# Modulation mat-vecs of a two-block network: one VectorE multiply-and-sum instruction per weight block in place of a GpSimd multiply and a ScalarE accumulating copy

## The chip, the cores and the metric

The kernel runs on one core of a Trainium2 chip. The metric is the device time of one execution in microseconds; the median of several runs is given.

## What is computed

Two transformer-like blocks over 512 tokens of width 1024, batch 1, all in float32. The first block has two layers of three sublayers (swiglu feed-forward, a mixer, swiglu feed-forward), the second has two layers (attention, then a squared-ReLU feed-forward) and carries 256 context tokens beside the 512. Every sublayer is modulated by columns that come from a conditioning vector:

```python
c_act = jax.nn.silu(c)
for l in range(DEPTH):                                   # first block
    mod = (c_act @ ada_w[l] + ada_b[l]).reshape(b, N_SUB, 3, 1, D_MODEL)
    h = modulate(x, mod[:, 0, 0], mod[:, 0, 1])          # x * (1 + scale) + shift
    y = swiglu_ffn(h, ffn1_w_in[l], ffn1_w_out[l])
    x = layer_norm(ALPHA * x + 0.5 * mod[:, 0, 2] * y, ln_g[l, 0], ln_b[l, 0])
    ...
for i in range(DEPTH):                                   # second block
    mod_lat = (silu_c @ w_ada[i] + b_ada[i])[:, None, :]
    mod_ctx = silu_cc @ w_ada[i] + b_ada[i]
    ...
```

A modulation vector of 1024 entries is one product of a vector with a 1024x1024 matrix. The change is about how these mat-vecs are computed.

## The kernel before

Activations lie feature-major: 1024 features are 8 tiles of 128 partitions by 512 tokens, kept as a pair of float32r parts (`hh`, `hl`) that add up to the float32 value. Every product is three matmuls (L322 to L324): high with high, high with low, low with high. Weights stream in blocks of 128x1024 float32 (512 KB): SyncE's queue issues the DMA into `raw`, ScalarE casts it to `hi` (L284), VectorE subtracts to get `lo` (L286; for a few blocks GpSimd does). The stream runs three blocks ahead of its use, with five places for split blocks.

The swiglu sublayers, FF1 to FF4 in order of time, have 22 tiles of hidden features in chunks of 2, 4, 4, 4, 4 and 4. A hidden tile takes two weight blocks and 48 matmuls into `pgu` (two PSUM tiles of two banks); ScalarE makes the silu `sg`, VectorE the product `gf` (the gate product), and `gf` is split into `gh` and `gl`. A chunk then goes through the output weights: eight `po` tiles (two PSUM banks), and for each a residual update `z` on VectorE (L635).

The modulation weights come as blocks `araw` of 128 output features by 1024 inputs. `ada` is a generator whose steps `ffn` takes between its hidden tiles. A step issues the DMA of one block from ScalarE's queue (L420, two buffers); for each conditioning vector that uses the block, GpSimd multiplies it with that vector, which lies on all partitions (`crow`), into `amul` (L425, one buffer), and ScalarE copies `amul` onto itself with a sum along the row, which gives one column of the result (L428). There are 224 blocks and 288 mat-vec steps: 56 of them in FF1, 80 in FF2, 88 in FF3 and 64 in FF4. In FF2 to FF4 some blocks of the second block's modulation serve two vectors (`mod` for the sequence, `modc` for the context).

The instructions' order on each engine is not the order of the code: the framework's scheduler sets it when the program is built. `after` adds an order between two instructions of one engine. `self.base` is the last instruction of the norm before, behind which the modulation steps must stay on their engine; before, it is the GpSimd instruction that makes the next residual base (L609).

Of the kernel before, what the change touches and what calls it, by code (L numbers as in the profile page):

```python
# [35 lines left out]
# ---------------------------------------------------------------- layout of the inputs (host, no arithmetic on data)  # L36

class Cols:
    """Small vectors, one array [128, n]: feature j * 128 + p of a vector sits in column off + j."""
# [16 lines left out]
def in_blocks(w):  # L56
    """(K, M) -> [M / 128][128][K / 128 * 128]: the stationary tiles of one block of output features."""
    k, m = w.shape
    return w.reshape(k // P, P, m // P, P).transpose(2, 1, 0, 3).reshape(m // P, P, k)


def out_blocks(w):
    """(chunk of K, 1024) -> [nb][128][1024]: for each block of output features, all k tiles of the chunk."""
    cs = w.shape[0] // P
    nm = KT // cs
    nb = KT // nm
    return w.reshape(cs, P, nb, nm, P).transpose(2, 1, 3, 0, 4).reshape(nb, P, DM)


def tok_blocks(w, kt):  # L70
    """(K, M) -> [K / 128 / kt][128][kt * M]: moving rows for token-major products."""
    k, m = w.shape
    n = k // P // kt
    return w.reshape(n, kt, P, m).transpose(0, 2, 1, 3).reshape(n, P, kt * m)
# [72 lines left out]
def ada_blocks(w):  # L147
    """(depth, 1024, M) -> [depth][M / 1024][8][128][1024]: output features on the partitions."""
# [113 lines left out]
# ---------------------------------------------------------------- the program  # L262

class WeightStream:
    """Streams blocks of weights in the order of their use and splits each exactly into two float32r parts."""
# [30 lines left out]
class Kernel:  # L296
# [3 lines left out]
    # ---------------- small helpers  # L300
# [11 lines left out]
    def split(self, hi, lo, src):  # L312
        """hi + lo = src exactly, both float32r."""
# [3 lines left out]
    def mm3(self, ps, terms, start=True, stop=True):  # L317
        """ps += sum of (a_hi + a_lo)^T (b_hi + b_lo) over the terms."""
# [7 lines left out]
    def dense(self, ps, w, off, x, ks, t0, t1):  # L326
        """ps[128 features, t0:t1] = W^T x for the stationary tiles at w[:, off + i * 128]."""
# [7 lines left out]
    def dense_tok(self, ps, blocks, kpb, m, x, ks, tb):  # L335
        """ps[128 tokens, m] = x^T W for the moving rows in blocks of kpb k tiles."""
# [9 lines left out]
    def quads(self, n, t, name, pool=None, tag="q4", bufs=4):  # L346
        """n pairs (hi, lo) of four feature tiles over t tokens."""
# [12 lines left out]
    def rows(self, t, name):  # L360
        """Eight float32 feature tiles over t tokens, as two groups of four."""
# [5 lines left out]
    def log_exp_table(self):  # L367
        """The activation tables that hold both the logarithm and the exponential, loaded at this point."""
# [3 lines left out]
    def after(self, ins, first):  # L372
        """Keeps ins behind first in their engine's order."""
# [3 lines left out]
    def rsqrt(self, pool, v, n, scale, eps, tag, make=None):  # L377
        """(scale * v + eps) ** -0.5 over [128, n], from logarithm and exponential with a Newton step."""
# [14 lines left out]
    def ps(self, tag, shape, name):  # L393
        """A tile in PSUM: tags a (two of one bank), b (two of two banks), c and d (one bank each)."""
# [6 lines left out]
    # ---------------- modulation  # L401

    def vector(self, row):
        """silu of one of the conditioning vectors, the same on all partitions."""
# [8 lines left out]
    def ada(self, src, vecs, first=None):  # L413
        """Work: src chunk @ silu(vector) + bias, as columns; vecs: list of (row, bias columns, factor, result)."""
        nc = self.nc
        rows = [self.vector(v[0]) for v in vecs]
        for j in range(KT):
# [5 lines left out]
            for row, (_, _, _, res) in zip(rows, vecs):  # L423
                m = self.apool.tile([P, DM], F32, tag="amul", bufs=1, name="amul")
                ins = nc.gpsimd.tensor_tensor(m, w, row, op=ALU.mult)  # L425
                if self.base:
                    self.after(ins, self.base)
                nc.scalar.activation(m, m, AF.Copy, accum_out=res[:, j : j + 1])  # L428
# [5 lines left out]
    def first_norm(self, z, g, b, src, bias):  # L434
        """The norm of the input and the first modulation, whose weights come block by block meanwhile.

        src: blocks of the shift (vector and tensor engines take one each) and of the scale, bias: their columns.
        """
# [23 lines left out]
        def mean(ps, x):  # L462
            """ps = mean of the eight tiles x(m)."""
# [52 lines left out]
    def mod_cols(self, g, b, shift, scale, name):  # L516
        """Columns that take the normalized rows to the next base (ALPHA x) and to the next modulated input."""
# [11 lines left out]
    # ---------------- layer norm (feature-major)  # L529

    def room(self):
        """Space for a norm beside the one that runs in the feed-forward sublayer's."""
        return (self.xpool or self.fpool).tile([P, 7, 256], F32, tag="lb", bufs=1, name="room")

    def layer_norm(self, z, t0, t1, eps, mod, h=None, final=None, behind=None):
        """The norm of z over [t0, t1) in place, in two steps, with the modulated result split into h."""
# [12 lines left out]
        def total(ps, rows, m, eng):  # L549
            """ps = mean over all features, as the rows of 1 or 2 feature tiles from m come in."""  # L550
# [30 lines left out]
        for m in range(KT):  # L581
# [27 lines left out]
            self.base = nc.gpsimd.tensor_scalar(zm, zm, ag, ab, op0=ALU.mult, op1=ALU.add)  # L609
# [4 lines left out]
    # ---------------- feed-forward sublayers  # L614

    def out_steps(self, parts, chunks, last=False, tag="a", before=None):
        """Work: z += gate * (W_out^T x) for chunks of k tiles; parts: (z, gate, x, t, result if not z),
        x one group of k tiles for each chunk.

        With last, by token halves, with before called ahead of each half of the first part.  # L620
        """
# [89 lines left out]
    def mlp(self, parts):  # L711
        """parts: (h, z, gate, t), the tokens of the sequence first, then those of the context, if any."""
# [10 lines left out]
        def inner(part, g, bl, fs):  # L723
            """Two hidden features of the tokens of the context."""
# [48 lines left out]
    # ---------------- mixer of the first block  # L773

    def mixer(self, l, h, out_first):
        nc, tc, ws = self.nc, self.tc, self.ws
        tt, stt, ts = nc.vector.tensor_tensor, nc.vector.scalar_tensor_tensor, nc.vector.tensor_scalar
        with tc.tile_pool(name="mx", bufs=1, reuse_waits="tile") as mp:
# [13 lines left out]
            # -- x B C: projection, causal convolution, silu  # L792
# [20 lines left out]
            # -- dt and f: softplus(u) = max(u, 0) + log1p(exp(-|u|)), token-major  # L813
# [1011 lines left out]
```

## Time and profile before

| | |
|---|---|
| median of 3 runs | 3942.31 us (3937.7 to 3942.68) |
| span of the profiled execution, first to last instruction | 3928.4 us |
| median less that span | 13.9 us |
| TensorE (PE) matmul busy | 3679.7 us, 20206 instructions |
| VectorE (DVE) busy | 2448.7 us |
| ScalarE (ACT) busy | 1843.0 us |
| GpSimd (POOL) busy | 1295.2 us |

The time of the profiled execution itself is not listed apart from the three runs; its span is, and the 13.9 us are what lies around it. A busy share is an average over stages with different limits, so it says where an engine's work is and not what the time hangs on; the chain of waits and the busy time of single stretches say that. Matmuls are pipelined: their rows overlap, and the count of matmuls in a stretch tells their pace better than their durations. PE is the matmul side of TensorE, PEld its weight loads, ACTq and SPq the queues from which ScalarE and SyncE issue DMAs.

### The profile page before, as it was taken

The page shows a single profiled execution, that of the slowest core. Times are in us where ns is not written, and L with a number is a line of the kernel's source. Part 1 is how long each engine was busy: PE and PEld are TensorE (multiplying, and loading weights), DVE is VectorE, ACT ScalarE, POOL GpSimd, SP SyncE. Part 2 cuts the span into 40 slices and gives each one's busy share as a digit, 9 for nine tenths or more (in the row PEclk, how much of TensorE's full clock was granted, in tenths as well). Part 3 has the DMA queues.
Part 4 walks back from the last instruction along what each step waited for, and adds up shares of the span by engine and source line. Part 5 has one row for each costly group of instructions (what it writes and reads, how often), then busy time and mean ns, then how long its engine had stood idle before and what let it go on. Part 6 is the DMA issues. An engine that isn't in the chain of part 4 may idle for free.

```text
span 3928.4 us, 51915 instructions
## 1 busy us (share of the span) xinstructions
PE 3679.7 (94%) x20206; PEld 3171.6 (81%) x20206; DVE 2448.7 (62%) x3699; ACT 1843.0 (47%) x3323; POOL 1295.2 (33%) x888
## 2 busy tenths in 40 slices
PE   7999999999989998989999888999999979989997
PEld 6788877888878887777888787888888868878886
DVE  7664666765676667577656778773333577875445
ACT  3552444555455554435543566452323366744332
POOL 5660313566566663146642212040000221122001
PEclk9999999999999999999999899999999989999998
DMA  6763223376445543124652111011211110112321
GB/s 217 226 221 108 89 68 106 124 233 205 141 153 191 171 129 107 60 97 145 198 194 67 38 38 54 24 54 60 65 60 64 54 58 30 39 49 76 97 92 59
DMA packets 125015, 418.47 MB, mean 107 GB/s; under 512 B 13336, under 2 KB 19224, under 8 KB 124768
## 3 DMA queue, kind: packets, MB, share of 16 engines
q1 hardware_dynamic: 90592, 293.50, 22.8%
q10 hardware_dynamic: 34176, 121.65, 9.6%
q8 instruction: 158, 2.59, 0.3%
q14 instruction: 89, 0.73, 0.1%
HBM read 404.62 MB, written 10.49 MB: 106 GB/s over the span
## 4 chain that ended last, share of the span: by engine, by line
PE 75%; DVE 12%; ACT 5%; POOL 4%; issue 4%; DMA 1%; POOLq 0%; SPq 0%; ACTq 0%; DVEq 0%
PE po L322 8%; PE po L323 8%; PE po L324 8%; PE pgu L323 7%; PE pgu L322 7%; PE pgu L324 7%; PE pm L323 3%; PE pm L322 3%; PE pm L324 3%; POOL amul L425 3%; PE pyo L1168 2%; PE ptt L1154 2%; PE psc L1319 1%; ACT hi L284 1%; DVE lo L286 1%
## 5 line engine op out<-in xcount | busy, mean ns | idle before, releaser
L286 DVE TENSOR_TENSOR lo<-raw,hi 128x1024 fp32r<-128x1024 f32 (+3 forms) x439 | 681.6, 1558 | 404.4 <-ACT hi L284 397.4
L284 ACT CAST hi<-raw 128x1024 fp32r<-128x1024 f32 (+2 forms) x502 | 514.8, 1029 | 861.3 <-PE po L323 455.5
L425 POOL TENSOR_TENSOR amul<-araw,crow 128x1024 f32<-128x1024 f32 x288 | 720.3, 2501 | 406.5 <-ACT amul L428 369.8
L635 DVE SCALAR_TENSOR_TENSOR z<-po,mod,z 128x512 f32<-128x512 f32 (+1 forms) x464 | 300.5, 655 | 489.9 <-PE po L324 488.6
L322 PE MATMUL pgu<-hh,hi 128*128 128x512 f32 (+1 forms) x1536 | 565.8, 373 | 14.6 <-DVE gf L671 6.7
L323 PE MATMUL pgu<-hl,hi 128*128 128x512 f32 (+1 forms) x1536 | 571.6, 373 | 6.1 <-DVE hl L608 4.3
L324 PE MATMUL pgu<-hh,lo 128*128 128x512 f32 (+1 forms) x1536 | 568.7, 371 | 1.9 <-DVE lo L286 1.8
L322 PE MATMUL po<-gh,hi 128*128 128x512 f32 (+1 forms) x1408 | 506.9, 366 | 11.9 <-DVE z L635 11.3
L323 PE MATMUL po<-gl,hi 128*128 128x512 f32 (+1 forms) x1408 | 510.2, 363 | 0.9 <-DVE gl L315 0.9
L324 PE MATMUL po<-gh,lo 128*128 128x512 f32 (+1 forms) x1408 | 509.5, 362 | 0.0
L428 ACT ACTIVATE amul<-amul 128x1024 f32<-128x1024 f32 x288 | 305.6, 1061 | 357.1 <-POOL amul L425 355.8
L286 POOL TENSOR_TENSOR lo<-raw,hi 128x1024 fp32r<-128x1024 f32 (+2 forms) x63 | 154.3, 2452 | 918.9 <-ACT hi L284 827.4
L322 PEld LDWEIGHTS pgu<-hh,hi 128*128 128x128 f32 x1536 | 292.6, 193 | 65.7 <-DVE gf L671 7.4
L323 PEld LDWEIGHTS pgu<-hl,hi 128*128 128x128 f32 x1536 | 295.1, 192 | 58.2 <-DVE hl L608 7.3
L324 PEld LDWEIGHTS pgu<-hh,lo 128*128 128x128 f32 x1536 | 295.5, 192 | 51.4 <-DVE lo L286 3.9
L322 PEld LDWEIGHTS po<-gh,hi 128*128 128x128 f32 x1408 | 268.5, 191 | 54.6 <-DVE z L635 14.6
L323 PEld LDWEIGHTS po<-gl,hi 128*128 128x128 f32 x1408 | 268.8, 191 | 40.6 <-DVE gl L315 1.8
L324 PEld LDWEIGHTS po<-gh,lo 128*128 128x128 f32 x1408 | 268.6, 191 | 40.0
L315 DVE TENSOR_TENSOR gl<-gf,gh 128x512 fp32r<-128x512 f32 (+1 forms) x158 | 165.7, 1051 | 139.6 <-ACT gh L314 139.4
L323 PE MATMUL pm<-hl,hi 128*128 128x512 f32 (+1 forms) x576 | 213.2, 371 | 6.2 <-DVE hl L608 3.9
L322 PE MATMUL pm<-hh,hi 128*128 128x512 f32 (+1 forms) x576 | 210.1, 370 | 4.5 <-ACT hi L284 1.8
L324 PE MATMUL pm<-hh,lo 128*128 128x512 f32 (+1 forms) x576 | 211.5, 370 | 1.8 <-DVE lo L286 1.8
(512 smaller groups left out, 7760.3 us busy)
## 6 DMA issues: line engine op xcount, KB each, us to landing
araw<-in_ada ACTq DMA_DIRECT2D x224, 512.0 KB, 3.5
raw<-in_w SPq DMA_DIRECT2D x128, 512.0 KB, 3.6
raw<-in_f1i SPq DMA_DIRECT2D x88, 512.0 KB, 4.4
raw<-in_f2i SPq DMA_DIRECT2D x88, 512.0 KB, 4.3
raw<-in_mi SPq DMA_DIRECT2D x48, 512.0 KB, 3.3
raw<-in_f1o SPq DMA_DIRECT2D x44, 512.0 KB, 4.3
raw<-in_f2o SPq DMA_DIRECT2D x44, 512.0 KB, 4.4
arawf<-in_ada SPq DMA_DIRECT2D x16, 512.0 KB, 8.6
```

The source lines that it names most:

```text
L284: nc.scalar.copy(hi[:, :n], raw[:, :n])
L286: eng.tensor_tensor(lo[:, :n], raw[:, :n], hi[:, :n].bitcast(F32), op=ALU.subtract)
L315: self.nc.vector.tensor_tensor(lo, src, hi.bitcast(F32), op=ALU.subtract)
L322: mm(ps, ah, bh, start=start and i == 0, stop=False)
L323: mm(ps, ah, bl, start=False, stop=False)
L324: mm(ps, al, bh, start=False, stop=stop and i == n - 1)
L425: ins = nc.gpsimd.tensor_tensor(m, w, row, op=ALU.mult)
L428: nc.scalar.activation(m, m, AF.Copy, accum_out=res[:, j : j + 1])
L635: nc.vector.scalar_tensor_tensor(to, ps, gate[:, m : m + 1], zm, op0=ALU.mult, op1=ALU.add)
L1154: nc.tensor.transpose(pt[:, k, r], pn[:, r, s], self.ident)
L1168: nc.tensor.matmul(out, v[:, kb], x, start=kb == 0 and i == 0, stop=kb == nkb - 1 and i == 1)
L1319: nc.tensor.matmul(ps[:, k0:k1], qt[:, q, q0 : q0 + P], kt[:, k0:k1], start=i == 0, stop=i == 1)
```

## The change

The GpSimd multiply and the ScalarE copy of each step become one `scalar_tensor_tensor` on VectorE: (block x 1.0) x vector, with the row sum written to the result's column. `amul` is still written and read by nobody. The DMA of the blocks stays on ScalarE's queue and keeps its two buffers. `self.base` becomes the VectorE instruction that makes the last low part `hl` of the norm, so that the order between norm and modulation holds on VectorE. Line numbers behind L425 rise by one, behind L609 by two.

```diff
@@ def ada
                 m = self.apool.tile([P, DM], F32, tag="amul", bufs=1, name="amul")
-                ins = nc.gpsimd.tensor_tensor(m, w, row, op=ALU.mult)
+                ins = nc.vector.scalar_tensor_tensor(
+                    m, w, 1.0, row, op0=ALU.mult, op1=ALU.mult, accum_out=res[:, j : j + 1]
+                )
                 if self.base:
                     self.after(ins, self.base)
-                nc.scalar.activation(m, m, AF.Copy, accum_out=res[:, j : j + 1])
@@ def layer_norm
-            self.base = nc.gpsimd.tensor_scalar(zm, zm, ag, ab, op0=ALU.mult, op1=ALU.add)
+            nc.gpsimd.tensor_scalar(zm, zm, ag, ab, op0=ALU.mult, op1=ALU.add)
+            self.base = lo
```

The scheduler orders the program anew. GpSimd and SyncE keep their order but for the multiplies that are gone. Three places show what moves.

VectorE at the start of FF1, behind the last low part `hl` of the first norm. Before:

```order
L286 TENSOR_TENSOR lo<-raw,hi 128x1024 x2
L671 TENSOR_TENSOR gf<-pgu,sg 128x512
L286 TENSOR_TENSOR lo<-raw,hi 128x1024
L315 TENSOR_TENSOR gl<-gf,gh 128x512
L286 TENSOR_TENSOR lo<-raw,hi 128x1024
L671 TENSOR_TENSOR gf<-pgu,sg 128x512
L315 TENSOR_TENSOR gl<-gf,gh 128x512
L286 TENSOR_TENSOR lo<-raw,hi 128x1024
L430 TENSOR_TENSOR mod_85<-mod_85,cols 128x8
```

The same place after the change:

```order
L425 SCALAR_TENSOR_TENSOR amul,mod_85<-araw,crow 128x1024 x6
L286 TENSOR_TENSOR lo<-raw,hi 128x1024
L425 SCALAR_TENSOR_TENSOR amul,mod_85<-araw,crow 128x1024
L286 TENSOR_TENSOR lo<-raw,hi 128x1024
L673 TENSOR_TENSOR gf<-pgu,sg 128x512
L425 SCALAR_TENSOR_TENSOR amul,mod_85<-araw,crow 128x1024
L286 TENSOR_TENSOR lo<-raw,hi 128x1024
L315 TENSOR_TENSOR gl<-gf,gh 128x512
L431 TENSOR_TENSOR mod_85<-mod_85,cols 128x8
L425 SCALAR_TENSOR_TENSOR amul,mod_85<-araw,crow 128x1024
```

Six multiplies stand ahead of the first weight split, and then about two beside each split.

VectorE in the middle of FF3, from one gate product to the next (the ones at 1220.40 and 1229.94 us in the trace of before). Before:

```order
L671 TENSOR_TENSOR gf<-pgu,sg 128x512
L286 TENSOR_TENSOR lo<-raw,hi 128x1024
L315 TENSOR_TENSOR gl<-gf,gh 128x512
L286 TENSOR_TENSOR lo<-raw,hi 128x1024 x2
L671 TENSOR_TENSOR gf<-pgu,sg 128x512
```

After, the first 12 of the 18 rows between the same two products:

```order
L673 TENSOR_TENSOR gf<-pgu,sg 128x512
L431 TENSOR_TENSOR modc<-modc,cols 128x8
L425 SCALAR_TENSOR_TENSOR amul,mod_86<-araw,crow 128x1024
L637 SCALAR_TENSOR_TENSOR z<-po,mod_85,z 128x512
L286 TENSOR_TENSOR lo<-raw,hi 128x1024
L315 TENSOR_TENSOR gl<-gf,gh 128x512
L425 SCALAR_TENSOR_TENSOR amul,modc<-araw,crow 128x1024
L637 SCALAR_TENSOR_TENSOR z<-po,mod_85,z 128x512
L425 SCALAR_TENSOR_TENSOR amul,mod_86<-araw,crow 128x1024
L425 SCALAR_TENSOR_TENSOR amul,modc<-araw,crow 128x1024
L286 TENSOR_TENSOR lo<-raw,hi 128x1024
L425 SCALAR_TENSOR_TENSOR amul,mod_86<-araw,crow 128x1024
```

Eight multiplies and three residual updates `z` now stand between the two products, where there were three splits and one `gl`.

ScalarE at the end of FF3, around the table load that opens the norm (`lnsg` and `lngf` are squares of that norm). Before:

```order
L428 ACTIVATE amul,mod_86<-amul 128x1024
L284 CAST hi<-raw 128x1024
L670 ACTIVATE sg<-pgu 128x256
L369 ACT_TABLE_LOAD
L314 CAST gh<-gf 128x256
L428 ACTIVATE amul,modc<-amul 128x1024
L284 CAST hi<-raw 128x1024
L428 ACTIVATE amul,mod_86<-amul 128x1024
L574 ACTIVATE lnsg<-z 128x512
L574 ACTIVATE lngf<-z 128x512
```

After:

```order
L284 CAST hi<-raw 128x1024
L672 ACTIVATE sg<-pgu 128x256
L369 ACT_TABLE_LOAD
L314 CAST gh<-gf 128x256
L284 CAST hi<-raw 128x1024
L575 ACTIVATE lnsg<-z 128x512
L575 ACTIVATE lngf<-z 128x512
```

The modulation steps that ran into the norm are no longer there; the last modulation DMA of FF3 stands some forty rows further up on ScalarE.

## Rows read from the trace of the kernel before

**Rows 1.** The page: busy time of each engine, and the chain of waits by line.

```profile
PE 3679.7 (94%) x20206; PEld 3171.6 (81%) x20206; DVE 2448.7 (62%) x3699; ACT 1843.0 (47%) x3323; POOL 1295.2 (33%) x888
...
PE 75%; DVE 12%; ACT 5%; POOL 4%; issue 4%; DMA 1%; POOLq 0%; SPq 0%; ACTq 0%; DVEq 0%
PE po L322 8%; PE po L323 8%; PE po L324 8%; PE pgu L323 7%; PE pgu L322 7%; PE pgu L324 7%; PE pm L323 3%; PE pm L322 3%; PE pm L324 3%; POOL amul L425 3%; PE pyo L1168 2%; PE ptt L1154 2%; PE psc L1319 1%; ACT hi L284 1%; DVE lo L286 1%
```

**Rows 2.** The page's groups: count | busy us, mean ns | idle before, releaser.

```profile
L284 ACT CAST hi<-raw 128x1024 fp32r<-128x1024 f32 (+2 forms) x502 | 514.8, 1029 | 861.3 <-PE po L323 455.5
L425 POOL TENSOR_TENSOR amul<-araw,crow 128x1024 f32<-128x1024 f32 x288 | 720.3, 2501 | 406.5 <-ACT amul L428 369.8
...
L428 ACT ACTIVATE amul<-amul 128x1024 f32<-128x1024 f32 x288 | 305.6, 1061 | 357.1 <-POOL amul L425 355.8
```

**Rows 3.** Busy time by stretches: PE, PEld, DVE, ACT, POOL; clock, DMA, GB/s.

```profile
300.00:400.00 100.00, 100.00 (x443) 82.90 (x442) 39.83 (x44) 26.46 (x31) 0.00 (x0) 1.00 0.32 103
...
1200.00:1300.00 100.00, 100.00 (x443) 82.86 (x442) 63.42 (x49) 54.98 (x83) 64.68 (x27) 1.00 0.57 186
```

**Rows 4.** The tile `amul`, first norm on VectorE: ns min/median/max, starts.

```profile
L498 DVE SCALAR_TENSOR_TENSOR amul<-arawf,crow x8: 1207/1212/3362, 15.2 to 55.7; 128x1024 f32<-128x1024 f32 x8
L498 DVE DVE_READ_ACCUMULATOR amul<-arawf,crow x8: 72/75/84, 16.3 to 56.9; 128x1 f32 x8
```

**Rows 5.** Timeline (start, us) of gate products on DVE and of `pxb` on PE.

```profile
87.64 0.69 DVE L671 TENSOR_TENSOR gf<-pgu,sg 128x512 f32<-128x512 f32 x1 [0.16 <-ACT sg L670]
403.52 0.69 DVE L671 TENSOR_TENSOR gf<-pgu,sg 128x512 f32<-128x512 f32 x1
445.52 0.50 PE L322 MATMUL pxb<-hh,hi 128*128 128x256 f32 x2
1126.34 0.68 DVE L671 TENSOR_TENSOR gf<-pgu,sg 128x512 f32<-128x512 f32 x1
1187.71 0.68 DVE L671 TENSOR_TENSOR gf<-pgu,sg 128x512 f32<-128x512 f32 x1
1220.40 0.68 DVE L671 TENSOR_TENSOR gf<-pgu,sg 128x512 f32<-128x512 f32 x1
1229.94 0.68 DVE L671 TENSOR_TENSOR gf<-pgu,sg 128x512 f32<-128x512 f32 x1
1316.64 0.68 DVE L671 TENSOR_TENSOR gf<-pgu,sg 128x512 f32<-128x512 f32 x1
1436.20 0.68 DVE L671 TENSOR_TENSOR gf<-pgu,sg 128x512 f32<-128x512 f32 x1
1485.93 0.58 PE L322 MATMUL pxb<-hh,hi 128*128 128x256 f32 x1 [4.36 <-ACT hh L607]
```

**Rows 6.** The tile `araw`, issue to landing, in 70:150 and then in 150:300.

```profile
DMA to landing us min/median/max: 3.1/3.4/4.7
...
DMA to landing us min/median/max: 3.2/4.1/5.9
```

**Rows 7.** Timeline of ScalarE and VectorE in FF1, 150 to 152 us.

```profile
150.21 1.06 ACT L428 ACTIVATE amul<-amul 128x1024 f32<-128x1024 f32 x1 [2.77 <-POOL amul L425]
...
151.26 0.58 ACT L670 ACTIVATE sg<-pgu 128x512 f32<-128x512 f32 x1
...
151.87 0.69 DVE L671 TENSOR_TENSOR gf<-pgu,sg 128x512 f32<-128x512 f32 x1 [3.94 <-ACT sg L670]
```

**Rows 8.** Waits of PE in 145:155: us in total, times, longest.

```profile
PE pgu L322 <- ACT hi L284: 3.2, 1, 3.2
```

**Rows 9.** Busy time right behind that wait, columns as in rows 3.

```profile
152.90:156.30 3.40, 3.32 (x7) 2.20 (x8) 2.58 (x2) 1.54 (x3) 2.10 (x2) 0.50 0.62 220
```

**Rows 10.** Groups of GpSimd in 1436:1486, the end of FF3.

```profile
L425 POOL TENSOR_TENSOR amul<-araw,crow 128x1024 f32<-128x1024 f32 x7 | 17.1, 2437 | 9.8 <-ACT amul L428 9.8
```

**Rows 11.** Timeline of the norm's first add at the ends of FF1 and FF3.

```profile
418.19 0.42 DVE L557 TENSOR_TENSOR lnsg<-z 128x256 f32<-128x256 f32 x1
...
1451.10 2.40 POOL L425 TENSOR_TENSOR amul<-araw,crow 128x1024 f32<-128x1024 f32 x1 [1.26 <-ACT amul L428]
1451.36 2.42 DVE L557 TENSOR_TENSOR lnsg<-z 128x256 f32<-128x256 f32 x1
```

## The prediction

> **What bounds the kernel now.** I read the page first: its shares of busy time, then the chain of waits. TensorE is busy for 3679.7 of 3928.4 us and holds 75% of the chain; GpSimd holds 4%, of which 3% are the multiply that the change removes [rows 1]. The groups of instructions give its size: 288 multiplies at 2.50 us on GpSimd and 288 accumulating copies at 1.06 us on ScalarE, each waiting for the other [rows 2]. So 720 us of GpSimd and 306 us of ScalarE go away, but a share is worth nothing until the stage is known. The multiplies run only inside the four swiglu sublayers of the first block (FF1 to FF4). The busy time by stretches decides there: in 300 to 400 us FF1 runs with no modulation work, in 1200 to 1300 us FF3 runs with it, and TensorE is at 100.00% with 443 matmuls in both [rows 3]. That is 0.2257 us a matmul either way. Inside such a stretch nothing can be gained. What is left is the few places where TensorE stood still because of this chain, and what can be lost is TensorE waiting for a VectorE that has become full.
>
> **The change part by part.**
>
> *The instruction itself.* The same form already stands in the first norm: 128x1024 multiply-and-sum on VectorE takes 1.207 us (least and median), its accumulator read 0.07 us, and the read starts before the multiply is over [rows 4]. I take 1.21 us. 288 of them are 348 us more on VectorE, which has 2448.7 us of 3928.4 [rows 1]. The maximum in that row, 3.36 us, ran beside GpSimd; in the stages in question GpSimd's only other work of weight is a few weight splits.
>
> The Trainium skill states against this in "Vector Engine (DVE) Microarchitecture Reference", section "Points that are easy to get wrong", that this instruction with two SBUF sources that are not bf16 runs at half throughput. The row of the first norm has just this case and does not show it: 1024 elements in 1.21 us, the price of the plain weight split of the same shape. By the page the term of 348 us would be about 700 us.
>
> *VectorE's budget.* Without modulation VectorE needs 39.83 us in 100 us [rows 3]; with GpSimd multiplying beside it, it shows 63.42 us for much the same work, so that contention leaves with the change. Now the order: over FF1 and FF2, once they have started, the built program puts 98 multiplies beside 51 weight splits, 1.92 for each. A weight block is 24 matmuls, 5.42 us, so one multiply in 2.82 us: 39.83% + 1.21/2.82 = 83% of VectorE. The densest stretch is in FF3, between the gate products that stand at 1187.71 and 1316.64 us before [rows 5]: 128.9 us, 61 multiplies, so 51.4 + 73.8 = 125.2 us, 97%. VectorE gets full but not over-full; on average it costs nothing, hidden by TensorE's own 100%.
>
> *Bursts.* In FF3 the products at 1220.40 and 1229.94 us are 9.5 us apart [rows 5], and the new order puts 8 multiplies (9.7 us), 4 splits, 3 residual updates, 2 gate products and a small one between them, about 18 us at uncontended durations: VectorE is some 8 us behind there. A gate product may be late by about 9.5 us (48 matmuls, 10.8 us, run before its PSUM tile is needed again, less 1.3 us for silu and product). A residual update may be late by 12 matmuls, 2.7 us, since `po` has two banks. So a burst costs nothing if only gate products are late, and up to 8 - 2.7 = 5.3 us if the updates are. I count four such bursts, smaller in FF2 and FF4: 0 to 15 us in all. I take 5 us, nearer to nothing, because the order lets matmuls of the next two features stand between those of `po`.
>
> *Waits for the weight blocks.* VectorE now waits itself for each 512 KB block, and behind a waiting multiply stand the splits, the residual updates and the gate products that TensorE waits for. The issue of a block's DMA on ScalarE's queue waits for the multiply two earlier (two buffers), and behind it stand the casts, the silu and the gate splits. A pair of multiplies so takes landing + 1.21 us at least. Landing has a median of 3.4 us in 70 to 150 us and 4.1 us in 150 to 300 us [rows 6]: 2.3 to 2.65 us a multiply, under the 2.82 us that the order asks for. It fits, narrowly. Price 0, upper bound below.
>
> *FF1: gain.* At 149.6 us TensorE stood still for 3.2 us: ScalarE waited 2.77 us for the GpSimd multiply, so silu came at 151.26 and the gate product at 151.87 [rows 7]; the wait is put down to another cast on ScalarE, released in the same run [rows 8]. Then the granted clock is 0.50, the lower of its two levels (1.2 GHz), over 152.9 to 156.3 us: 7 matmuls in 3.4 us where 15 fit, 1.8 us lost [rows 9]. Together 5.0 us. As a whole: from the first to the 21st gate product FF1 takes 403.52 - 87.64 = 315.9 us, FF3 1436.20 - 1126.34 = 309.9 us [rows 5], the same work. Gain 5.0 to 6.0; I take 6.0, since ScalarE no longer waits on GpSimd anywhere in it.
>
> *The end of FF3: gain.* FF1 and FF3 both end in a norm and a mixer. From the 21st gate product to the first `pxb` matmul FF1 takes 445.52 - 403.52 = 42.0 us, FF3 1485.93 - 1436.20 = 49.7 us [rows 5]. In FF3 the 88 multiplies, one in about 3.8 us (2.50 us, and 369.8 / 288 = 1.28 us of waiting for the copy [rows 2]), have not ended by then: 7 still run on GpSimd, and a norm add of VectorE takes 2.42 us beside one of them where it takes 0.42 us in FF1 [rows 10, 11]. In the new order nothing of this stands there any more. FF3's end should cost what FF1's does: 7.7 us gained. If the order of matmuls makes less of it, 5.
>
> Sum: -6.0 - 7.7 + 5 = -8.7 us. The span goes from 3928.4 to about 3920 us. What lies around the span is 3942.3 - 3928.4 = 13.9 us and stays; against the median of 3942.3 us that is **3934 us**. After FF4 no modulation work runs, and the rest of the program keeps its order but for a few matmuls.
>
> **The rivals.**
>
> *A. The bursts eat the gain.* Updates are late at every burst, 15 us: -13.7 + 15 = +1 us, 3944 us. For it: 97% load in FF3 on an in-order queue, and z updates stand behind two to three multiplies. Against it: before, VectorE idled 37 us in 100 in FF3 [rows 3], and the contention that leaves gives back 63.4 - 39.8 = 23.6 us in 100, some 70% of what the 27 multiplies of that stretch take (33 us).
>
> *B. Slower: VectorE and ScalarE wait for each other's DMA step.* If the DMA issue regularly stands behind one cast on ScalarE (1.03 us [rows 2]) and landing is 4.1 us, a pair takes 4.1 + 1.03 + 1.21 = 6.3 us, 3.17 us a multiply against the 2.82 us asked for. It decides from landing plus issue delay of 2 x 2.82 - 1.21 = 4.4 us on. Then 0.35 us x (98 in FF1 and FF2 + 56 single ones in FF3 and FF4) = 54 us, less 2.7 us of tolerance in each of four sublayers = 43 us; with the gains +29: 3971 us. For it: new traffic is denser, and landing already rises from 3.4 to 4.1 us. Against it: the casts mostly wait for TensorE, not the other way round, and the order keeps several DMA issues together.
>
> *C. The instruction takes twice its time* beside the other work of the sublayers, 2.42 us: then VectorE needs 0.398 x 2.82 + 2.42 = 3.54 us for every 2.82 us of TensorE and becomes the bound, 0.72 us x 288 = 207 us; 3942 + 207 - 14 = 4135 us. The row of the first norm speaks against it [rows 4]. (This is what the page's rule would do here.)
>
> *D. No bursts at all*: 3928.6 us.
>
> **How the numbers follow.** About 0.2% (8 us, so 3934.4 to 3950.2) is what a measurement of this kernel can tell from no change. Forecast and D together 0.47, all just faster by more than that; A, and half of it, 0.33 (no difference); B 0.18 and C 0.02, slower. Likeliest: 3934 us. Range: D less 2 us below, 3926; above through A and into B, where half of its waits come true with little tolerance, 3965. Less than a tenth lies beyond each end.
>
> **What would show it.** Right: TensorE at 443 matmuls in 100 us inside FF1 to FF4; no multiply on GpSimd or after about 1320 us in FF3; first to 21st gate product at 310 us in FF1; FF3's end at 42 us; multiply-and-sum at 1.2 us and splits back at 1.2 us. Wrong: TensorE waiting for VectorE's residual updates in FF3 (A), VectorE idle in front of `amul` for `araw` DMAs and FF1 or FF2 longer than 316 us (B), or the instruction at 2.4 us (C).

## The result, and the profile after

The changed kernel takes 3970.84 us (median of 4 runs, 3967.09 to 3974.56), the kernel before 3940.01 us in the runs that stand beside it (3929.82 to 3942.68). The ratio is 1.0084, 95% interval 1.0072 to 1.0097: slower by 31 us, where 8 us faster was forecast. 3971 us is the number of rival B.

The profiled execution took 3974.56 us with a span of 3972.8 us, so 1.8 us lie around a span. The page of the changed kernel, the lines that answer to [rows 1]:

```profile
PE 3701.6 (93%) x20206; PEld 3179.2 (80%) x20206; DVE 2513.5 (63%) x4275; ACT 1526.3 (38%) x2747; POOL 577.1 (15%) x600
...
PE 67%; DVE 16%; DMA 7%; ACT 4%; issue 4%; POOL 1%; ACTq 0%; DVEq 0%; SPq 0%; POOLq 0%
PE po L322 8%; PE po L323 7%; PE po L324 7%; DMA araw<-in_ada 7%; PE pgu L323 5%; PE pgu L322 5%; PE pgu L324 5%; PE pm L323 3%; PE pm L322 3%; PE pm L324 3%; DVE amul L425 3%; PE pyo L1170 2%; PE ptt L1156 2%; DVE lo L286 2%; ACT hi L284 1%
```

The work went where it was meant to go: GpSimd lost 718 us and ScalarE 317 us. But TensorE's share of the chain fell from 75% to 67%, and a line stands in it that was not among the chain's lines before: the DMA of the modulation blocks, `araw`, with 7%. Its multiply is in the chain too, on VectorE instead of GpSimd.

The page's groups show the price of the instruction and what stood ahead of it (busy us, mean ns | idle us before it, what ended most of that idle time):

```profile
L286 DVE TENSOR_TENSOR lo<-raw,hi 128x1024 fp32r<-128x1024 f32 (+3 forms) x439 | 534.6, 1221 | 343.9 <-ACT hi L284 338.2
...
L425 DVE SCALAR_TENSOR_TENSOR amul<-araw,crow 128x1024 f32<-128x1024 f32 x288 | 351.7, 1221 | 123.5 <-DMA araw<-in_ada 120.9
```

The multiply-and-sum costs 1.221 us, as predicted (351.7 us in all against 348). In front of it VectorE stood idle for 120.9 us until a block had landed. The busy time by stretches, columns as in [rows 3], with one more stretch of FF1:

```profile
100.00:200.00 100.00, 93.81 (x398) 75.58 (x397) 77.58 (x119) 22.09 (x26) 0.00 (x0) 0.97 0.79 263
300.00:400.00 100.00, 100.00 (x442) 82.78 (x442) 42.31 (x46) 27.09 (x31) 0.00 (x0) 1.00 0.32 106
1200.00:1300.00 100.00, 94.64 (x410) 76.15 (x409) 90.19 (x142) 24.37 (x29) 0.00 (x0) 1.00 0.70 227
```

Where no modulation runs (300 to 400 us) TensorE still does 442 matmuls in 100 us. Where it runs, it does 398 and 410 in place of the full 443. In the first stretch VectorE is busy for 77.6 of 100 us only: it is not full, it waits.

The gate products of FF1 and FF3 on VectorE, and the first `pxb` matmul behind FF3 (start, duration in us), answer to [rows 5]:

```profile
88.28 0.68 DVE L673 TENSOR_TENSOR gf<-pgu,sg 128x512 f32<-128x512 f32 x1
...
412.45 0.68 DVE L673 TENSOR_TENSOR gf<-pgu,sg 128x512 f32<-128x512 f32 x1
...
1154.08 0.68 DVE L673 TENSOR_TENSOR gf<-pgu,sg 128x512 f32<-128x512 f32 x1
...
1471.83 0.68 DVE L673 TENSOR_TENSOR gf<-pgu,sg 128x512 f32<-128x512 f32 x1
...
1513.93 0.58 PE L322 MATMUL pxb<-hh,hi 128*128 128x256 f32 x1 [4.36 <-ACT hh L608]
```

From two such rows for each sublayer (the last two columns are of experiments told below):

| us | before | after | no loading (e1) | late (e9) |
|---|---|---|---|---|
| FF1, first to 21st gate product | 315.9 | 324.2 | 310.3 | 311.1 |
| FF2 | 310.2 | 326.2 | 309.2 | 308.9 |
| FF3 | 309.9 | 317.7 | 310.5 | 308.1 |
| FF4 | 311.0 | 324.5 | 310.3 | 309.6 |
| end of FF3, 21st gate product to `pxb` | 49.7 | 42.1 | 42.1 | 43.3 |

The four sublayers lost 45.6 us and the end of FF3 gave back 7.6 us; the other 6.4 us by which the two spans differ lie between and behind these stretches and were not followed up. The trace also tells in what the 45.6 us consist. In these four stretches the idle time of TensorE, summed over its rows, goes from 8.1 to 37.5 us, in 21 waits of over 0.5 us where there were 6. The time at a granted clock of 0.50 with TensorE at work goes from 6.2 to 38.3 us, and half of such time is lost. 29.4 + 16.0 = 45.4 us. (The two spans differ by 44.4 us and the medians by 30.8. The profiled execution of before was one of its shortest, 3928.4 + 1.8 = 3930.2 us against a median of 3940; that of the changed kernel was the longest of its four.)

What TensorE waited for between 100 and 1990 us (us in total, times, longest):

```profile
PE pgu L322 <- ACT hi L284: 25.0, 10, 5.5
PE po L322 <- DVE z L637: 20.0, 14, 2.8
...
PE pgu L322 <- DVE gf L673: 8.7, 3, 4.3
```

The first row had one event of 3.2 us before [rows 8]. Most of the other two was there before the change too:

```profile
PE po L322 <- DVE z L635: 17.7, 7, 3.1
...
PE pgu L322 <- DVE gf L671: 6.7, 3, 4.3
```

What is new is that TensorE waits for the cast of a weight block on ScalarE, an engine that the change made emptier. One of the two longest of these waits, in FF2, shows why. ScalarE and its DMA queue between 806 and 821 us (start, duration, engine; in brackets the idle time before and what ended it):

```profile
806.34 0.62 ACT L314 CAST gh<-gf 128x512 fp32r<-128x512 f32 x1 [3.92 <-DVE gf L673]
807.47 0.34 ACTq L420 DMA_DIRECT2D araw<-in_ada  x1
807.93 1.05 ACT L284 CAST hi<-raw 128x1024 fp32r<-128x1024 f32 x1 [0.97 <-DVE amul L425]
809.22 7.76 ACTq L420 DMA_DIRECT2D araw<-in_ada  x3
817.08 1.04 ACT L284 CAST hi<-raw 128x1024 fp32r<-128x1024 f32 x1 [8.09 <-DVE amul L425]
```

VectorE in the same stretch:

```profile
809.11 1.22 DVE L286 TENSOR_TENSOR lo<-raw,hi 128x1024 fp32r<-128x1024 f32 x1
812.17 1.23 DVE L425 SCALAR_TENSOR_TENSOR amul<-araw,crow 128x1024 f32<-128x1024 f32 x1 [1.84 <-DMA araw<-in_ada]
...
815.38 1.22 DVE L425 SCALAR_TENSOR_TENSOR amul<-araw,crow 128x1024 f32<-128x1024 f32 x1 [1.97 <-DMA araw<-in_ada]
...
818.15 1.23 DVE L286 TENSOR_TENSOR lo<-raw,hi 128x1024 fp32r<-128x1024 f32 x1 [1.54 <-ACT hi L284]
```

And TensorE:

```profile
818.17 0.80 PE L322 MATMUL pgu<-hh,hi 128*128 128x512 f32 x1 [5.38 <-ACT hi L284]
```

Three DMA issues stand in a row on ScalarE from 809.22 on. The second and the third each need a buffer that a multiply still has to free (the ones at 812.17 and 815.38), and each of these multiplies stands until its own block has landed. So ScalarE is idle for 8.1 us before the cast behind the issues, and TensorE stands for 5.4 us. Within that wait the clock falls to the lower of its two levels (1.2 GHz), and it stays there beyond the wait's end, 6.8 us in all; columns as in [rows 9]:

```profile
815.60:822.40 6.80, 4.19 (x9) 2.89 (x10) 5.26 (x9) 2.16 (x3) 0.00 (x0) 0.50 0.59 196
```

Issue to landing of the blocks, in 70 to 150 us and in 150 to 300 us, which answers to [rows 6]:

```profile
DMA to landing us min/median/max: 3.1/4.4/6.5
...
DMA to landing us min/median/max: 3.2/4.4/5.8
```

The median is 4.4 us in both, where it was 3.4 and 4.1.

### The profile page after: what moved, and what is told of

Its sections match the earlier page's. It is cut to its first block, busy times and chain, and to the rows that moved or that the text cites. A ratio compares the mean times of both kernels' runs of the same rounds, so it can differ in the third digit from the quotient of the medians.

```text
span 3972.8 us, 51826 instructions
## 1 busy us (share of the span) xinstructions
PE 3701.6 (93%) x20206; PEld 3179.2 (80%) x20206; DVE 2513.5 (63%) x4275; ACT 1526.3 (38%) x2747; POOL 577.1 (15%) x600
## 4 chain that ended last, share of the span: by engine, by line
PE 67%; DVE 16%; DMA 7%; ACT 4%; issue 4%; POOL 1%; ACTq 0%; DVEq 0%; SPq 0%; POOLq 0%
PE po L322 8%; PE po L323 7%; PE po L324 7%; DMA araw<-in_ada 7%; PE pgu L323 5%; PE pgu L322 5%; PE pgu L324 5%; PE pm L323 3%; PE pm L322 3%; PE pm L324 3%; DVE amul L425 3%; PE pyo L1170 2%; PE ptt L1156 2%; DVE lo L286 2%; ACT hi L284 1%
## 5 line engine op out<-in xcount | busy, mean ns | idle before, releaser
L286 DVE TENSOR_TENSOR lo<-raw,hi 128x1024 fp32r<-128x1024 f32 (+3 forms) x439 | 534.6, 1221 | 343.9 <-ACT hi L284 338.2
L322 PE MATMUL po<-gh,hi 128*128 128x512 f32 (+1 forms) x1408 | 505.9, 365 | 14.4 <-DVE z L637 13.9
L425 DVE SCALAR_TENSOR_TENSOR amul<-araw,crow 128x1024 f32<-128x1024 f32 x288 | 351.7, 1221 | 123.5 <-DMA araw<-in_ada 120.9
L315 DVE TENSOR_TENSOR gl<-gf,gh 128x512 fp32r<-128x512 f32 (+1 forms) x158 | 105.2, 668 | 120.4 <-ACT gh L314 120.3
L315 DVE TENSOR_TENSOR pt<-ptt,pt 128x384 fp32r<-128x384 f32 (+1 forms) x272 | 149.1, 558 | 36.2 <-ACT pt L314 31.6
```

The costliest lines, as they stand in the source:

```text
L286: eng.tensor_tensor(lo[:, :n], raw[:, :n], hi[:, :n].bitcast(F32), op=ALU.subtract)
L315: self.nc.vector.tensor_tensor(lo, src, hi.bitcast(F32), op=ALU.subtract)
L322: mm(ps, ah, bh, start=start and i == 0, stop=False)
L425: ins = nc.vector.scalar_tensor_tensor(m, w, 1.0, row, op0=ALU.mult, op1=ALU.mult, accum_out=res[:, j : j + 1])
```

## The experiments

Three theories could make the loss. **W**: VectorE stands in front of a multiply until its block has landed, and what TensorE needs stands behind it. **L**: VectorE is simply too full in the dense stretches. **H**: the denser block traffic delays the weight stream itself. Each ratio is to the kernel before on the same chip.

**e1, no loading.** The kernel leaves out the loading of the blocks: the multiplies read a resident vector, times 0.

```diff
-            w = self.apool.tile([P, DM], F32, tag="araw", bufs=2, name="araw")
-            dma = nc.scalar.dma_start(w, src[j])
-            if first:
-                self.after(dma, first)
...
-                    m, w, 1.0, row, op0=ALU.mult, op1=ALU.mult, accum_out=res[:, j : j + 1]
+                    m, rows[0], 0.0, row, op0=ALU.mult, op1=ALU.mult, accum_out=res[:, j : j + 1]
```

> Leaves out the loading of the modulation blocks: each of the 288 multiplies reads the vector that is resident instead of a block, with a factor 0, so the modulation is the bias alone. VectorE's work is unchanged (288 multiplies of about 1.22 us), and the built order is as dense as before or denser (6 to 8 multiplies between two gate products of one chunk where the changed kernel has 6). Theory W (VectorE stands in front of a multiply until its block has landed, and what TensorE needs stands behind it): without landing there is nothing to wait for; first to 21st gate product about 310 us in each of FF1 to FF4 (324.2, 326.2, 317.7, 324.5 in the changed kernel), about 3928 us, ratio to before 0.997. Theory L (VectorE is over-full in the dense stretches, whatever it waits for): the order is no thinner, so FF1 and FF2 stay above 320 us and the time stays at 3960 to 3975, ratio 1.005 to 1.009. Theory H (the denser block traffic makes the weight stream's own blocks late): as W, 3928.

Measured: 3927.75 us, ratio 0.9968 (0.9955 to 0.9981). VectorE has all its 288 multiplies, and the four stretches take 309.2 to 310.5 us. L falls. The end of FF3, on VectorE and then on TensorE:

```profile
1442.72 0.68 DVE L669 TENSOR_TENSOR gf<-pgu,sg 128x512 f32<-128x512 f32 x1
...
1484.80 0.58 PE L322 MATMUL pxb<-hh,hi 128*128 128x256 f32 x1 [4.37 <-ACT hh L604]
```

42.1 us. Without the loading the whole loss is gone, and both gains that the prediction named are there. This run takes away the wait and the block traffic together (W and H); the next ones part them.

**e2, narrow multiplies.** The kernel leaves out 960 of the 1024 columns of each multiply. All blocks are loaded and waited for; VectorE's own work on them nearly vanishes.

```diff
-                    m, w, 1.0, row, op0=ALU.mult, op1=ALU.mult, accum_out=res[:, j : j + 1]
+                    m[:, :64], w[:, :64], 1.0, row[:, :64], op0=ALU.mult, op1=ALU.mult, accum_out=res[:, j : j + 1]
```

> Leaves out most of each multiply: it works on 64 of the 1024 columns, so the modulation is wrong, while all 224 blocks of 512 KB are still loaded and waited for. Theory W: the two-buffer ring (issue, landing 4.4 us, multiply) still sets the pace of VectorE's queue, and the built order is denser (9 to 10 multiplies between two gate products in places), so much of the loss stays: first to 21st gate product 315 to 330 us in FF1 and FF2, 3945 to 3970 us, ratio 1.001 to 1.008. Theory L: 288 x 1.1 us of VectorE are gone, so 310 us everywhere and about 3928 us, ratio 0.997. Theory H: as long as the changed kernel or longer, 3970, with raw landing above 5 us.

Measured: 3961.16 us, ratio 1.0059 (1.0040 to 1.0077); 316.1 to 322.4 us in the four stretches. VectorE's waits, us in total, times, longest:

```profile
DVE amul L425 <- DMA araw<-in_ada: 252.4, 183, 4.2
```

With a fifth of the instruction's time (0.225 us) 29.4 of the 45.6 us that the four stretches lost stay. So the waiting costs without the work. Its length does not measure the loss, though: VectorE waits twice as long here as in the changed kernel (252.4 against 120.9 us), and less is lost. H has no support either: issue to landing of `raw` in 60 to 300 us has a median of 4.4 us here, 4.7 in the changed kernel, 4.6 before.

**e3, paced.** Each block's DMA stays behind the silu of the hidden tile after which its step is taken.

```diff
-            if first:
-                self.after(dma, first)
+            if first or self.silu:
+                self.after(dma, first or self.silu)
```

> One order more: the DMA of each modulation block is kept behind the silu of the hidden tile after which its step is taken, so the built order has 3 to 6 multiplies between two gate products all through the first 18 hidden tiles in place of 6 to 15 in the first ten. W, L and H all ask for less per stretch here, so this doesn't tell them apart; it tells whether the density is the cause at all. If it is: 310 to 313 us from first to 21st gate product in FF1 and FF2, 3925 to 3938 us, ratio 0.996 to 0.9995. If the loss were in the instruction itself (its price beside other work) or in the norm's order, it would stay at 3960 to 3975.

Measured: 3947.26 us, ratio 1.0019 (1.0007 to 1.0031): a miss. FF1 and FF4 came down to 311.5 and 312.3 us, FF3 to 315.5, FF2 stayed at 327.0. VectorE in FF2 there:

```profile
809.93 1.23 DVE L425 SCALAR_TENSOR_TENSOR amul<-araw,crow 128x1024 f32<-128x1024 f32 x1 [1.68 <-DMA araw<-in_ada]
...
812.90 1.23 DVE L425 SCALAR_TENSOR_TENSOR amul<-araw,crow 128x1024 f32<-128x1024 f32 x1 [1.73 <-DMA araw<-in_ada]
...
814.05 1.41 DVE L637 SCALAR_TENSOR_TENSOR z<-po,mod,z 128x512 f32<-128x512 f32 x2
```

Two residual updates stand behind multiplies that wait, and TensorE waits 4.5 us for them. The steps of one hidden tile are still issued together, and two buffers can't cover them: thinning the work on average is not enough. FF1 shows it as well: it asks for only one multiply in 5.1 us here, and VectorE still waits 47.4 us for its blocks (36.5 in the changed kernel), though FF1 takes only 1.1 us more than without loading.

**e4, three buffers.**

```diff
-            w = self.apool.tile([P, DM], F32, tag="araw", bufs=2, name="araw")
+            w = self.apool.tile([P, DM], F32, tag="araw", bufs=3, name="araw")
...
```

(A second place that uses the same buffers has the same edit.)

> Three buffers for the modulation blocks in place of two. Theory W: the ring carries three blocks for each landing of 4.4 us, 1.9 us a multiply and no longer 2.8 to 3; VectorE's wait for landing falls from 121 us to under 50 us, and half or more of the loss goes: 3935 to 3955 us, ratio 0.999 to 1.004. Theory L: the built order is denser (7 multiplies between two gate products in places), VectorE is fuller still: 3970 to 3985 us, ratio 1.008 to 1.012. Theory H: denser traffic, same or longer than the changed kernel, and raw landing above 5 us.

Measured: 3935.6 us, ratio 0.9993 (0.9983 to 1.0003), with VectorE as busy as in the changed kernel and its order denser. Its waits:

```profile
DVE amul L425 <- DMA araw<-in_ada: 45.2, 45, 1.9
```

121 us became 45, and the loss against the kernel before is gone; the four stretches still take 10.7 us more than without loading (e1). L and H both asked for at least the changed kernel's time here, so W holds against them. The Trainium skill, in "Trainium Kernel Development and Optimization", section "Best Practices", advises double buffering to overlap DMA with compute. This kernel had two buffers and shows the limit of that rule: with two of them 121 us of waiting, with three 45.

**e5, the DMAs on GpSimd's queue,** two buffers. Is it ScalarE's queue (WA) or VectorE's (WV) on which the wait does harm?

```diff
-            dma = nc.scalar.dma_start(w, src[j])
+            dma = (nc.scalar if first else nc.gpsimd).dma_start(w, src[j])
```

> The DMAs of the modulation blocks (all but FF1's first eight) are issued from GpSimd's queue in place of ScalarE's, still with two buffers. The earlier runs put the loss on waiting for the blocks; this tells two places of that wait apart. Theory WA (ScalarE's queue: a DMA issue that waits for its buffer holds the casts and the silu behind it, so TensorE waits for a cast, 25.0 us at 10 places in the changed kernel): that wait falls under 5 us, and the time to 3935 to 3948 us, ratio 0.999 to 1.002. Theory WV (VectorE's queue: the multiply that waits for landing holds splits, residual updates and gate products): VectorE's wait for blocks stays above 100 us and TensorE's waits move to VectorE's results; 3955 to 3968 us, ratio 1.004 to 1.007.

Measured: 3978.88 us, ratio 1.0105 (1.0086 to 1.0124). TensorE's waits for the cast are gone (0.7 us left of 25.0), and as long a wait for the split has come (28.3 us in 7 waits). TensorE, in the same place of FF2:

```profile
822.81 0.80 PE L324 MATMUL pgu<-hh,lo 128*128 128x512 f32 x1 [4.73 <-DVE lo L286]
```

VectorE just before, where the split that ends this wait stands behind two multiplies that wait for blocks:

```profile
810.03 1.23 DVE L425 SCALAR_TENSOR_TENSOR amul<-araw,crow 128x1024 f32<-128x1024 f32 x1 [4.12 <-DMA araw<-in_ada]
...
818.23 1.22 DVE L425 SCALAR_TENSOR_TENSOR amul<-araw,crow 128x1024 f32<-128x1024 f32 x1 [0.64 <-DMA araw<-in_ada]
...
820.38 1.23 DVE L425 SCALAR_TENSOR_TENSOR amul<-araw,crow 128x1024 f32<-128x1024 f32 x1 [0.92 <-DMA araw<-in_ada]
...
821.53 1.22 DVE L286 TENSOR_TENSOR lo<-raw,hi 128x1024 fp32r<-128x1024 f32 x1
```

So WA falls: the stalled issue on ScalarE is where the wait was seen, not what it hangs on. With that queue free, the order on VectorE shows a wait of the same size. The time is beyond both expectations; the interval overlaps that of the changed kernel, so a further rise is not sure. The move to GpSimd's queue also has a price of its own: 21 us with three buffers (e6 against e4). If it costs as much here, e5 without it would stand at some 3958 us, an estimate, which is still above WA's range and within WV's. The page of this kernel lists the moved transfers as another kind:

```profile
q0 software_dynamic: 31104, 113.26, 8.2%
```

An issue takes 0.527 us on GpSimd, 0.334 us on ScalarE. The Trainium skill, in "SBUF — State Buffer", section "SBUF: two separate sides", says that the descriptors of such a DMA are made by GpSimd, and that it can't write them while VectorE runs an operation that holds the ports the two share (its example is a float32 copy within SBUF). No run here shows whether the multiplies and splits of this kernel do that, or separates it from the longer issue.

**e6, three buffers and GpSimd's queue.** The edits of e4 and e5 together.

> Three buffers and issue from GpSimd's queue together: neither queue should be held. If the two waits are all of the loss, it is like the kernel without loading: 3924 to 3932 us, ratio 0.996 to 0.998, VectorE's wait for blocks under 40 us, and first to 21st gate product 309 to 312 us in FF1 to FF4. If a third cause (VectorE's load, DMA traffic) is left, it stays at or above the 3936 us of three buffers alone.

Measured: 3956.62 us, ratio 1.0047 (1.0033 to 1.0062): a miss, worse than three buffers alone. VectorE's wait for blocks is 64.4 us with a longest of 6.6 us (45.2 and 1.9 in e4), and landing takes up to 11.2 us (7.1 in e4). Late landings alone do not explain it: in e7, on ScalarE's queue, landing takes up to 8.7 us and nothing is lost against e4. Why GpSimd's queue is slower stays open, here as in e5.

**e7, three buffers and paced.** The edits of e3 and e4 together.

> Three buffers and the pacing by the silu together. Pacing alone left 146 us of VectorE's waiting for blocks and 11.1 us of TensorE's waiting for residual updates in FF2. If what was left there is the two-buffer ring, it goes: 3924 to 3932 us, ratio 0.996 to 0.998, no TensorE wait above 2 us in FF2. If pacing itself is harmful (DMA issues that come late behind a silu), FF2 stays above 318 us from first to 21st gate product and the time at 3940 or more.

Measured: 3935.23 us, ratio 0.9993 (0.9984 to 1.0002). FF1 and FF4 take 309.6 and 310.2 us, FF2 and FF3 still 315.6 and 315.0, with three waits of 1.5 to 2.2 us for residual updates in FF2. The time lies between the two expectations, and neither holds. VectorE still waits 83.6 us for blocks: pacing the DMA alone doesn't keep the multiply away from its landing.

**e8, half the change.** VectorE multiplies, ScalarE still sums.

```diff
-                ins = nc.vector.scalar_tensor_tensor(
-                    m, w, 1.0, row, op0=ALU.mult, op1=ALU.mult, accum_out=res[:, j : j + 1]
-                )
+                ins = nc.vector.tensor_tensor(m, w, row, op=ALU.mult)
...
+                nc.scalar.activation(m, m, AF.Copy, accum_out=res[:, j : j + 1])
```

> Only half of the change: the multiply goes to VectorE, the accumulating copy stays on ScalarE. Two buffers and ScalarE's queue as before. VectorE multiplies as long as in the changed kernel, ScalarE has its 306 us back, and since one copy follows each multiply the built order is thinner (4 to 5 multiplies between two gate products in place of 6 or more). Theory W: the wait stays where it was, with less asked for per stretch: 3945 to 3962 us, ratio 1.002 to 1.006, VectorE's wait for blocks above 80 us. If what costs is the lost ScalarE copy or the accumulating form of the instruction itself, it is like the kernel before or better: 3930 to 3942, ratio under 1.0005.

Measured: 3940.85 us, ratio 1.0012 (1.0000 to 1.0024); the ratio lies between those of the two expectations, and VectorE waits 91.0 us for blocks, as W asked for. The copy that seemed to be pure cost keeps the steps apart (one per 3.05 us in FF1, 2.88 in the changed kernel), which may be what took most of the harm away; this was not shown by itself. The run doesn't decide between the two.

**e9, late.** If waiting for landing is all, a multiply that stands far enough behind its DMA should cost nothing. Three buffers, steps over 20 hidden tiles, each DMA behind the gate product's cast, each multiply behind a later gate product:

```diff
+            while len(self.pend) >= (3 if self.gates else 2):
+                self.pend.pop(0)()
-            w = self.apool.tile([P, DM], F32, tag="araw", bufs=2, name="araw")
+            w = self.apool.tile([P, DM], F32, tag="araw", bufs=3, name="araw")
             dma = nc.scalar.dma_start(w, src[j])
-            if first:
-                self.after(dma, first)
+            if first or self.gates:
+                self.after(dma, first or self.gates[-1][0])
...
+            def mults(w=w, j=j, k=len(self.gates)):
...
+                    if len(self.gates) > k or self.base:
+                        self.after(ins, self.gates[-1][1] if len(self.gates) > k else self.base)
...
+            self.pend.append(mults)
...
-        left = sum(FFN_CHUNKS[:-1])
+        left = sum(FFN_CHUNKS) - 2
...
+                self.gates.append((cast, prod))
...
```

> Three buffers, the steps spread over 20 of the 22 hidden tiles, each block's DMA kept behind the cast of the gate product of its hidden tile, and its multiply kept behind a later hidden tile's gate product (some 10 us, where landing took 4.4 to 4.7 us). So a block should have landed when VectorE comes to its multiply. If waiting for landing is all that the change cost: VectorE's wait for blocks falls under 25 us, first to 21st gate product is 309 to 312 us in FF1 to FF4, and the time is that of the kernel without loading, 3924 to 3932 us, ratio 0.996 to 0.9985. If the DMA issue, which now waits for its buffer on ScalarE's queue, holds the casts as it did in the changed kernel: TensorE waits for casts, FF2 and FF4 above 315 us, 3935 to 3950 us.

Measured: 3914.98 us, ratio 0.9945 (0.9932 to 0.9959). It beats the kernel before by 22 us and the changed one by 56, and came out 9 us under the range expected. VectorE's waits and then, from the page, the chain:

```profile
DVE amul L429 <- DMA araw<-in_ada: 8.0, 10, 1.5
```

```profile
PE 79%; DVE 12%; ACT 4%; issue 3%; POOL 1%; DMA 1%; SPq 0%; POOLq 0%; DVEq 0%; ACTq 0%
```

The stretches of FF1 and FF3 that lost matmuls in the changed kernel:

```profile
100.00:200.00 100.00, 100.00 (x443) 82.81 (x442) 61.73 (x89) 26.79 (x32) 0.00 (x0) 1.00 0.61 198
...
1200.00:1300.00 100.00, 100.00 (x442) 82.79 (x442) 72.03 (x108) 27.06 (x34) 0.00 (x0) 1.00 0.60 193
```

TensorE is full in both. Landing has not become faster (median 4.5 us); it is only no longer waited for. Against e4 the ratio fell from 0.9993 to 0.9945, and three things changed: the spread over 20 hidden tiles, the place of the DMA and the place of the multiply. Spreading and pacing the DMAs with three buffers gained nothing (e7), which points at the multiply's place; no run changes that alone.

**e10, the same spreading with GpSimd and ScalarE.** Is it the VectorE instruction or the spreading that gained? The edit against e9 (`self.base` is GpSimd's again, too):

```diff
-                    ins = nc.vector.scalar_tensor_tensor(
-                        m, w, 1.0, row, op0=ALU.mult, op1=ALU.mult, accum_out=res[:, j : j + 1]
-                    )
-                    if len(self.gates) > k or self.base:
-                        self.after(ins, self.gates[-1][1] if len(self.gates) > k else self.base)
+                    ins = nc.gpsimd.tensor_tensor(m, w, row, op=ALU.mult)
+                    if self.base:
+                        self.after(ins, self.base)
+                    nc.scalar.activation(m, m, AF.Copy, accum_out=res[:, j : j + 1])
...
```

> The previous kernel (three buffers, steps spread over 20 hidden tiles, DMA behind the cast) with the multiply back on GpSimd and the sum on ScalarE, as before the change. It tells how much of the 0.55% that the previous kernel gained belongs to the VectorE instruction and how much to the spreading alone. Theory 1 (VectorE's instruction is worth the gains the prediction named, once it doesn't wait): GpSimd at about 3.8 us a step needs 88 x 3.8 = 334 us for FF3, more than FF3's 310 us, so the end of FF3 stays late (49 us or more from the 21st gate product to the next matmul of the mixer, where 42 to 43 is undisturbed) and FF1 keeps a stall: 3930 to 3945 us, ratio 0.998 to 1.002. Theory 2 (the spreading did it): 3912 to 3922 us, ratio 0.994 to 0.996.

Measured: 4019.93 us, ratio 1.0229 (1.0198 to 1.0259), far slower than either theory gave. GpSimd's waits:

```profile
POOL amul L429 <- ACT amul L432: 336.0, 243, 4.4
POOL amul L429 <- DMA araw<-in_ada: 316.7, 36, 28.5
```

Its two engines wait for each other as before, and now for blocks whose DMAs start later. FF1 takes 338.8 us from first to 21st gate product and the end of FF3 49.2 us; the extent of FF1's loss was not followed up. The four stretches lose 40 us against the kernel before. As much again is lost between the sublayers: from FF2's 21st gate product to FF3's first 95.7 us in place of 70.5, from FF3's to FF4's 368.5 in place of 351.5, and GpSimd's multiplies run on for some 77 and 89 us behind these 21st products. At its pace the steps of FF2 and FF3 don't end with the sublayer once they are spread over it. Spreading is not a gain by itself. The VectorE instruction, with its 1.2 us, is what can be spread.

## Why the prediction was wrong, point by point

- **The instruction** and **VectorE's budget** were right: 1.221 us against 1.21, the splits back at 1.221 us, and VectorE's work alone costs TensorE nothing (e1). The Trainium skill's half throughput for this instruction ("Vector Engine (DVE) Microarchitecture Reference", "Points that are easy to get wrong") did not show beside all the other work either: rival C is out.
- **The gains** were right. Without waiting FF1 takes 310.3 us (-5.6; -6.0 forecast) and the end of FF3 42.1 us (-7.6; -7.7 forecast). The end of FF3 gave its 7.6 us in the changed kernel too.
- **Bursts**: 5 us taken, upper bound 15. In e1, with bursts as dense, FF3 takes 310.5 us, 0.6 us more than before. Rival D, no bursts, gave 3928.6 us, 0.9965 of the 3942.3 us that it was counted from; e1's ratio is 0.9968. This term was too large: in e1's four stretches TensorE has no wait of over 0.5 us for a residual update.
- **Waits for the weight blocks** is the step that failed. It compared a ring of landing + 1.21 us for two blocks, 2.3 to 2.65 us a multiply, with the 2.82 us that the order asks for, wrote "it fits, narrowly", and priced it at 0. Landing came out at 4.4 us under the new traffic, so the ring takes (4.4 + 1.22) / 2 = 2.81 us: no slack at all. FF1 ran one step per 2.88 us. Without slack a late landing is waited for on VectorE and on ScalarE's queue, where the rows behind it are the ones TensorE needs. Measured price: +45.6 us over the four sublayers against the kernel before, against 0 (52.3 us against e1, which has the gains). An average period was also too coarse a measure: in e3's FF1 it is 5.1 us, far above the ring's, and VectorE still waits, because the issues of one hidden tile stand together. The prediction had the threshold in its hands (B decides "from landing plus issue delay of 4.4 us on") and took the median of the old traffic for the new one.
- **Rival B** had the number, 3971 us, and half of the mechanism. Its signs came true: VectorE stands in front of `amul`, and FF1 and FF2 take more than 316 us. ScalarE's queue is held by DMA issues, too. But e5 shows that ScalarE's part isn't needed for the loss. B's 43 us are near the 45.6 us found, by luck: the losses came in 21 waits of 0.5 to 5.5 us and in stretches at the lower clock, which no term of B contained and which made up 16 of the 45 us.
- **What lies around the span** was mis-sized, ahead of the prediction too: 1.8 us, not 13.9. The rest of the 13.9 us was the difference between one short execution and the median. It changed no sign.
- The chance of 0.18 for B was too low for a term whose bound stood at 0.2 us a step from its threshold.

## What to carry to other kernels

When a transfer's consumer moves to another engine, the wait for the transfer moves with it. Ask what stands behind the consumer on its new engine, and compare the ring's period (landing under the new traffic + use, over the number of buffers) with the period that the order asks for, where the steps stand closest and not on average; equality was a loss here, not a fit. A slow helper engine that waits alone may be cheaper than a fast one that makes a critical queue wait. Before giving up the faster form, put its use well behind its load: here three buffers removed the loss, and three buffers with a spread and later place in the order turned 0.84% slower into 0.55% faster.

## What the runs showed that was not expected

- DMAs moved to GpSimd's queue, nearly idle in these sublayers, were worse by 21 us with three buffers (ratio 1.0047 against 0.9993, e6 and e4), with landings of up to 11.2 us. The cause is not settled.
- Executions of one kernel on one chip differ by 10 to 20 us with the mean granted clock: of e1's ten, the span was 3913.5 us at 0.978 and 3932.7 us at 0.972. A single trace should be set against its own execution's time, not against the median.
- The waits cost more than their length. With four waits of TensorE of 2.6 to 5.4 us in FF1 and FF2 went stretches of 3.4 or 6.8 us at the lower clock; over the four sublayers 29.4 us more of waiting came with 16.0 us more of loss by the clock.
